# Feed-forward input as seven block products instead of eight: 19 gate/up pairs of a decoder layer in Strassen form

## The chip, the cores and the metric

One core of a Trainium2 chip runs the whole program. TensorE (PE in the profile) does the matmuls, VectorE (DVE) and ScalarE (ACT) the elementwise work, GpSimd (POOL) almost nothing, SyncE (SP) issues most DMAs. Matmuls write into PSUM, eight banks of 128 x 512 fp32 numbers; everything else lies in SBUF. Each engine works through its own queue in order and waits for others by semaphores. The metric is device time in microseconds.

## The reference

One hybrid decoder layer, fp32, 512 positions, width 1024: three token mixers, an output projection, and a gated feed-forward layer. The change touches the last, together with the norm ahead of it:

```
x = x + rms_norm(merged @ w_o, g_post_mix)
hf = rms_norm(x, g_pre_ffn)                        # 512 x 1024
f_gate, f_up = split(hf @ w_ffn_in, 2, axis=-1)    # 2816 columns each
f = (silu(f_gate) * f_up) @ w_ffn_out              # 2816 -> 1024
return x + rms_norm(f, g_post_ffn)
```

## The kernel before

Every large product is done in three passes: each fp32 operand is split into a high part in the matmul format fp32r and a low part (the rest), and high x high, high x low and low x high are summed in a bank. `split` (L114, L119) is a ScalarE copy into the high part and a VectorE subtraction for the low one. Weights come 128 x 1024 at a time: one DMA into a staging buffer, one split, then a unit of hi and lo tiles. `wlist` holds all weights in order, and `unit()` keeps three loaded ahead.

The program is written as Python generators that `run` interleaves; Tile, the layer below, then orders each engine's instructions by a model of its own and places the waits. The tail of the program runs so:

- `wo_pass` / `wo_norm` (L1014, L1027 to L1055): output projection for two of four row chunks at a time, then norm, residual, second norm, and four transposes per group through two `tr` banks into the transposed activations fh and fl. The second half of the norm runs while the next stage has begun.
- `ffn_head`: three gate/up pairs in two column halves, 256 of the 512 positions at a time, so that the first half can start before the norm of the second is done. 24 matmuls per unit and half.
- `ffn_tile`, 19 times: one pair, that is 128 gate and 128 up columns. 24 matmuls of 512 columns for the gate, 24 for the up part (8 blocks of the inner dimension x 3 passes, L212), each with its own weight load, in two banks. Then `ffn_out`: ScalarE Silu of the gate bank, VectorE product with the up bank, and a split of the result f.
- `down` (L1116): the output product, 22 units, with f as the loaded operand. It ends in `close`, which needs x for the residual.

Of the kernel before, what the change touches and what calls it, by code (L numbers as in the profile page):

```python
# [29 lines left out]
S = 512  # L30
# [20 lines left out]
def hybrid_block(ctx: ExitStack, tc: tile.TileContext, A, out):  # L51
# [23 lines left out]
    def next_phase(i):  # L75
        if phase[0]:
            phase[0].__exit__(None, None, None)
        phase[0] = tc.tile_pool(name=f"phase{i}", bufs=1, reuse_waits="tile")
# [16 lines left out]
    def row(name, dt=F32, tag="row"):  # L95
        return mid.tile([128, S], dt, tag=tag, name=nm(name), bufs={"row": 6, "q32": 2, "tg": 2}[tag])

# [61 lines left out]
    HEAD, LAST, LASTV = 3, 4, 2  # L159
    wlist += [(A["w_fi"][i], "h" if i < 4 else None) for i in range(2 * NFF)]  # L160
    wlist += [(A["w_fo"][i], "y" if 22 - LAST <= i < 20 else None) for i in range(22)]
    wready = {}
# [3 lines left out]
    def wload(upto):  # L166
        while wnext[0] < min(upto, len(wlist)):
            i = wnext[0]
# [38 lines left out]
    def passes(ps, hi, lo, xh, xl, m=128, n0=0, n1=S):  # L207

        t = 0
        for k in range(NK):  # L210
            for w, x in ((hi, xh), (hi, xl), (lo, xh)):
                res["mm"] = PE.matmul(ps[:m, n0:n1], w[:, k * 128:k * 128 + m], x[k][:, n0:n1], start=(t == 0),  # L212
                          stop=(t == 3 * NK - 1))
                t += 1
                if t % 6 == 0 and t < 3 * NK:
                    yield
# [742 lines left out]
    def gate_part(b, j):  # L959
        ps = bank("mm")  # L960
        yield from matrix(ps, hh, hl)
        t = row("tg", tag="tg")
        mg[b, j] = t
        SC.activation(t, ps, AF.Tanh, scale=0.5)
# [20 lines left out]
    def rows_in():  # L985
        gb = slab("gb", tag="gb", shape=(2, D))
        res["gb"] = gb
        SC.dma_start(gb[:, 0], bass.AP(tensor=A["grow"].tensor, offset=A["grow"].offset, ap=[[0, 128], [1, D]]))
        SC.dma_start(gb[:, 1], bass.AP(tensor=A["grow"].tensor, offset=A["grow"].offset + D,
                                       ap=[[0, 128], [1, D]]))  # L990
        V.tensor_scalar(gb[:, 0], gb[:, 0], 0.5, None, op0=OP.mult)
        xs = [slab("xr", tag="x", shape=(2, D)) for _ in range(2)]
        for i in range(2):
            SC.dma_start(xs[i], A["x"][:, 2 * i:2 * i + 2, :])
        res["x"] = [xs[c // 2][:, c % 2, :] for c in range(4)]
        res["ss"] = const.tile([128, 4, 4], F32, name="ss")
        res["fh"], res["fl"] = Pair("fh", F32R, "y"), Pair("fl", F32R, "y")

# [20 lines left out]
    def wo_norm(c0):  # L1019
# [24 lines left out]
        for _ in range({0: 9, 2: 14}[c0]):  # L1044
            yield 1
        for c in cs:
            for f in range(2):
# [5 lines left out]
                with tc.issue_after(res["mm"].ins):  # L1053
                    for i in range(4):
                        PE.transpose(pt[:, i * 128:(i + 1) * 128], n[:, i * 128:(i + 1) * 128], ident)  # L1055
                q = slice(c * 128, (c + 1) * 128)
                split(pt.rearrange("p (k t) -> p k t", k=4), res["fh"].t[f][:, :, q], res["fl"].t[f][:, :, q])
                for _ in range({0: 1, 2: 2}[c0]):
                    yield 1

    ff = {"h": [], "l": []}

    def ffn_out(j, pg, pu):

        if j % 2 == 0:
            ff["t"] = slab("f", F32R, (["m"] * 2 + ["mo"] * 4 + ["f"] + ["h"] * 4)[j // 2], (2, 2, S))
        ff["h"].append(ff["t"][:, j % 2, 0, :])
        ff["l"].append(ff["t"][:, j % 2, 1, :])
        s = row("silu")
        res["silu"] = SC.activation(s, pg, AF.Silu)  # L1070
        V.tensor_mul(s, s, pu)  # L1071
        split(s, ff["h"][j], ff["l"][j])

    def ffn_head(n):

        us, bs = [], []
        for i in range(2 * n):
            us.append(unit())
            bs.append(bank("mm"))
            yield from passes(bs[i], *us[i], res["fh"], res["fl"], n1=256)  # L1080
            yield
        for i in range(2 * n):
            yield from passes(bs[i], *us[i], res["fh"], res["fl"], n0=256)
            yield
            if i % 2:
                ffn_out(i // 2, bs[i - 1], bs[i])

    def ffn_tile(j):
        pg, pu = bank("mm"), bank("mm")
        yield from matrix(pg, res["fh"], res["fl"])  # L1090
        yield
        yield from matrix(pu, res["fh"], res["fl"])
        ffn_out(j, pg, pu)

    def down(f, last):
# [49 lines left out]
        for i in range(n - last):  # L1145
            hi, lo = unit()
            for c in range(4):
                block(c, i, hi, lo)
                yield
# [172 lines left out]
```

## Time and profile before

| | |
|---|---|
| median of 3 runs | 1148.39 us (1148.23 to 1148.74) |
| profiled execution: span, first to last instruction | 1146.6 us |
| busy: TensorE / its weight loads | 1133.5 us (99%) / 945.5 us (82%) |
| busy: VectorE / ScalarE / GpSimd | 689.8 us (60%) / 533.3 us (47%) / 24.0 us (2%) |
| 19 gate/up pairs, 813.35 to 1020.10 us | 206.75 us |

Each number on the page is one execution, and the span leaves out what lies around the instructions: 1.8 us between it and the median of the runs. In a group row the count stands behind the x, then busy time and mean time of one, then how long the engine stood idle ahead of them and for whom. Rows of a timeline begin with start and duration in us. A matmul's duration covers its way through the array; its successor starts before it ends, so the rate is read from the starts.

### The profile page before, as it was taken

What the parts mean: (1) busy time and instruction counts of PE and PEld (TensorE: products, weight loads), DVE (VectorE), ACT (ScalarE), POOL (GpSimd) and SP (SyncE); (2) the same over time, 40 slices, a digit from 0 to 9 for tenths busy, and PEclk for the clock granted to TensorE, in tenths of its full rate; (3) what the DMA queues carried; (4) which work ended last, traced back from release to release, by engine and by line L of the source; (5) the groups of instructions that cost most, each with busy time, mean ns of one, the idle gap of its engine ahead of it and who ended that gap; (6) DMA issues with size and microseconds to landing.
All of it is one profiled execution on the core that took longest, in us unless ns stands there. A gap on an engine that the chain in (4) does not pass through costs nothing.

```text
span 1146.6 us, 14314 instructions
## 1 busy us (share of the span) xinstructions
PE 1133.5 (99%) x5528; PEld 945.5 (82%) x5528; DVE 689.8 (60%) x1284; ACT 533.3 (47%) x934; POOL 24.0 (2%) x39
## 2 busy tenths in 40 slices
PE   9999999999999999999999999999999999999997
PEld 8888788888889888888788788889888888888886
DVE  5975968362675999989997734466333333332323
ACT  6746656132344787767777433343322232231221
POOL 1000022200000000000000000000000000000000
PEclk9999999999999999999999999999999999999999
DMA  8332223422223101111021432431223323332332
GB/s 314 100 109 74 92 92 112 182 83 101 86 80 93 59 34 56 56 56 56 19 74 56 149 127 92 141 114 40 74 92 101 101 92 93 105 115 92 95 108 73
DMA packets 30163, 108.61 MB, mean 95 GB/s; under 512 B 3536, under 2 KB 3824, under 8 KB 28944
## 3 DMA queue, kind: packets, MB, share of 16 engines
q1 hardware_dynamic: 27648, 97.98, 26.1%
q10 hardware_dynamic: 2160, 9.04, 2.2%
q8 instruction: 43, 0.70, 0.3%
q0 software_dynamic: 288, 0.69, 0.2%
q14 instruction: 24, 0.20, 0.1%
HBM read 105.60 MB, written 2.10 MB: 94 GB/s over the span
## 4 chain that ended last, share of the span: by engine, by line
PE 90%; DVE 6%; ACT 3%; DMA 1%; issue 1%; SPq 0%; DVEq 0%; ACTq 0%
PE mm L212 59%; PE mm L1116 10%; PE mm L496 3%; PE sc L808 3%; PE o L846 3%; PE tr L833 3%; PE mm L724 2%; PE mm L1014 2%; DVE lo L119 1%; PE tr L422 1%; DVE ti L449 1%; DMA raw<-in_w_v 1%; PE tr L556 1%; PE tr L640 1%; PE tr L746 1%
## 5 line engine op out<-in xcount | busy, mean ns | idle before, releaser
L114 ACT ACTIVATE hi<-raw 128x1024 fp32r<-128x1024 f32 (+1 forms) x162 | 170.8, 1054 | 352.6 <-PE mm L212 161.3
L119 DVE TENSOR_TENSOR lo<-raw,hi 128x1024 fp32r<-128x1024 f32 (+1 forms) x162 | 197.8, 1221 | 211.2 <-ACT hi L114 204.1
L212 PE MATMUL mm<-hh,hi 128*128 128x512 f32 x504 | 199.7, 396 | 0.0
L212 PE MATMUL mm<-hl,hi 128*128 128x512 f32 x504 | 197.4, 392 | 0.0
L212 PE MATMUL mm<-hh,lo 128*128 128x512 f32 x504 | 197.4, 392 | 0.0
L212 PE MATMUL mm<-fh,hi 128*128 128x512 f32 (+1 forms) x336 | 127.6, 380 | 0.0
L212 PE MATMUL mm<-fl,hi 128*128 128x512 f32 (+1 forms) x336 | 127.3, 379 | 0.0
L212 PE MATMUL mm<-fh,lo 128*128 128x512 f32 (+1 forms) x336 | 127.3, 379 | 0.0
L212 PEld LDWEIGHTS mm<-hh,lo 128*128 128x128 f32 x504 | 94.6, 188 | 19.7 <-issue 0.2
L212 PEld LDWEIGHTS mm<-hh,hi 128*128 128x128 f32 x504 | 94.7, 188 | 19.0 <-ACT hi L114 0.4
L212 PEld LDWEIGHTS mm<-hl,hi 128*128 128x128 f32 x504 | 94.7, 188 | 18.5 <-issue 0.2
L1116 PE MATMUL mm<-hi,f 128*128 128x512 f32 x320 | 99.2, 389 | 0.0
L814 ACT ACTIVATE P<-P,ast 128x128 f32<-128x128 f32 (+3 forms) x128 | 70.6, 554 | 23.1 <-DVE ast L812 22.5
L212 PEld LDWEIGHTS mm<-fl,hi 128*128 128x128 f32 x336 | 63.2, 188 | 11.9
L212 PEld LDWEIGHTS mm<-fh,lo 128*128 128x128 f32 x336 | 63.2, 188 | 11.9
L212 PEld LDWEIGHTS mm<-fh,hi 128*128 128x128 f32 x336 | 63.2, 188 | 11.7
L1116 PEld LDWEIGHTS mm<-hi,f 128*128 128x128 f32 x320 | 60.1, 188 | 12.4
L812 DVE CUSTOM_DVE_ANT_0 P<-sc,mask 128x128 f32<-128x128 f32 (+3 forms) x128 | 57.8, 483 | 8.3 <-PE sc L808 7.4
L1116 PE MATMUL mm<-lo,f 128*128 128x512 f32 x160 | 62.2, 389 | 0.0
L114 ACT ACTIVATE ph<-tr 128x512 fp32r<-128x512 f32 x80 | 46.9, 591 | 26.4 <-PE tr L833 25.5
L1071 DVE TENSOR_TENSOR silu<-silu,mm 128x512 f32<-128x512 f32 x22 | 15.1, 688 | 70.9 <-PE mm L212 70.9
L119 DVE TENSOR_TENSOR pl<-tr,ph 128x512 fp32r<-128x512 f32 x80 | 54.3, 685 | 2.9 <-PE o L846 1.0
(298 smaller groups left out, 1907.3 us busy)
## 6 DMA issues: line engine op xcount, KB each, us to landing
raw<-in_w_in SPq DMA_DIRECT2D x64, 512.0 KB, 3.5
raw<-in_w_fi SPq DMA_DIRECT2D x44, 512.0 KB, 3.5
raw<-in_w_br SPq DMA_DIRECT2D x24, 512.0 KB, 3.4
raw<-in_w_fo SPq DMA_DIRECT2D x22, 512.0 KB, 3.5
w<-in_cw ACTq DMA_DIRECT2D x4, 1024.0 KB, 5.0
raw<-in_w_o SPq DMA_DIRECT2D x8, 512.0 KB, 3.5
raw<-in_w_v SPq DMA_DIRECT2D x7, 512.0 KB, 5.2
xt<-in_xT SPq DMA_DIRECT2D x8, 256.0 KB, 6.7
```

What stands on the lines that cost most here:

```text
L114: SC.activation(hi, src, AF.Copy)
L119: res["lo"] = V.tensor_sub(lo, src, f32(hi))
L212: res["mm"] = PE.matmul(ps[:m, n0:n1], w[:, k * 128:k * 128 + m], x[k][:, n0:n1], start=(t == 0), stop=(t == 3 * NK - 1))
L496: res["mm"] = PE.matmul(b[c], x[k][:, c * 128:(c + 1) * 128], w[:, kk * 512:kk * 512 + 512], start=(k == 0 and t == 0), stop=(k == NK - 1 ...
L724: PE.matmul(ps, x[k][:, q], w[:, ws], start=(k == 0 and t == 0), stop=(k == NK - 1 and t == 2))
L808: PE.matmul(ps[:, :w * n].rearrange("p (b n) -> p b n", b=w), lhs, K[:, i, brs[0]:brs[-1] + 1, :n], start=(i == 0), stop=(i == 1))
L812: V.tensor_tensor_reduce(out=t, in0=ps[:, b * n:b * n + n], in1=mask[0][:, S - n:], scale=-0.125, scalar=3.0e38, op0=OP.add, op1=OP.min, a ...
L814: SC.activation(t, t, AF.Exp, scale=-1.0, bias=st[:, 0, j, b:b + 1], accum_out=st[:, 1, j, b:b + 1])
L833: PE.transpose(pt[:, j * 128:(j + 1) * 128], self.part(j, br)[:, kt * 128:(kt + 1) * 128], ident)
L846: PE.matmul(po, VV[:, kt, g % 2, br].rearrange("p i d -> p (i d)"), x, start=(br == 0 and kt == 0 and t == 0), stop=(br == 1 and kt == a a ...
L1014: res["mm"] = PE.matmul(b[c, f], x[k][:, q], w[:, fs], start=(k == 0 and t == 0), stop=(k == NK - 1 and t == 2))
L1116: PE.matmul(b[c], x[k][:, q], w[:, ws], start=(k == 0 and t == 0), stop=(k == NFF - 1 and t == 2))
```

## The change

Let the activations be a 2 x 2 block matrix A (position halves of 256 by inner halves of 512) and a pair's weights a 2 x 2 block matrix B (inner halves by gate and up). The product A B by blocks takes eight block products; the change computes it with seven (Winograd's form of Strassen's scheme): P1 to P7, each 512 inner x 256 positions x 128 columns, with block sums S1 to S4 of A (made once) and T1 to T4 of B (made for each pair). A product is 4 inner blocks x 3 passes = 12 matmuls of 256 columns. P1, P6, P5 and P3 add up in one bank, and P7 and P4 in another, P2 has a third. ScalarE copies the first bank after P1 (a), after P1+P6 (b) and after P1+P6+P5 (d), so that the four results are a + P2, b + P7 + P4, d + P7, and the bank itself.

The core of the diff:

```diff
+                if c0 == 0:
+                    SC.activation(F[f][:, :, q], p3, AF.Copy)
+                elif f == 0:
+                    SC.activation(F[2][:, :, q], p3, AF.Copy)
+                else:
+                    V.scalar_tensor_tensor(F[3][:, :, q], p3, -1.0, F[2][:, :, q], op0=OP.mult, op1=OP.subtract)
...
+        spill()
+        V.tensor_sub(F[2], F[0], F[2])
+        yield 1
+        V.scalar_tensor_tensor(F[0], F[3], -1.0, F[0], op0=OP.mult, op1=OP.subtract)
+        yield 1
+        V.tensor_sub(F[1], F[1], F[0])
+        yield 1
+        prep.load(HEAD)
+        prep.load(HEAD + 1)
+        for n, f in (("S3", 2), ("S2", 0), ("S1", 3), ("S4", 1)):
+            res[n] = slab(n, F32R, "mo", (2, 4, 256))
+            split(F[f], res[n][:, 0], res[n][:, 1])
+            yield 1
+        for step in prep.steps(HEAD):
+            step()
...
-    def ffn_out(j, pg, pu):
-        if j % 2 == 0:
-            ff["t"] = slab("f", F32R, (["m"] * 2 + ["mo"] * 4 + ["f"] + ["h"] * 4)[j // 2], (2, 2, S))
-        ff["h"].append(ff["t"][:, j % 2, 0, :])
-        ff["l"].append(ff["t"][:, j % 2, 1, :])
-        s = row("silu")
-        res["silu"] = SC.activation(s, pg, AF.Silu)
-        V.tensor_mul(s, s, pu)
-        split(s, ff["h"][j], ff["l"][j])
...
+            def b_pair():
+                split(r[0], *g["B11", "B21"])
+            def t13():
+                V.tensor_sub(T[:, 0], B["B11"], B["B12"])
+                V.tensor_sub(T[:, 1], B["B22"], B["B12"])
+            def t24():
+                V.tensor_add(T[:, 2], B["B22"], T[:, 0])
+                V.tensor_sub(T[:, 3], B["B21"], T[:, 2])
+            def s13():
+                split(T[:, 0:2, :].rearrange("p a n -> p (a n)"), *g["T1", "T3"])
+            def s22():
+                split(B["B22"], *g["B22"])
+            def s24():
+                split(T[:, 2:4, :].rearrange("p a n -> p (a n)"), *g["T2", "T4"])
...
+    PRODUCTS = {"P1": ("B11", (0, 0)), "P2": ("B21", (0, 1)), "P3": ("B22", "S4"), "P4": ("T4", (1, 1)),
+                "P5": ("T1", "S1"), "P6": ("T2", "S2"), "P7": ("T3", "S3")}
...
+            first = p in ("P1", "P7", "P2")
+            if first:
+                d[p] = bank("mm")[:, :256]
+            ps = d[{"P6": "P1", "P5": "P1", "P3": "P1", "P4": "P7"}.get(p, p)]
+            for k in range(4):
+                ks = slice(k * 128, k * 128 + 128)
+                for t, (w, l) in enumerate(((hi, 0), (hi, 1), (lo, 0))):
+                    res["mm"] = PE.matmul(ps, w[:, ks], x[:, l, k, :], start=(first and k == t == 0),
+                                          stop=(k == 3 and t == 2), skip_group_check=not first)
...
+        def keep(j, n):
+            SC.activation(st[j][n], st[j]["P1"], AF.Copy)
...
+            if name == "P1":
+                rows(j)
+                keep(j, "a")
+            elif name == "P6":
+                keep(j, "b")
+            elif name == "P5":
+                keep(j, "d")
+            elif name == "C11":
+                V.tensor_add(d["a"], d["a"], d["P2"])
+                SC.activation(d["a"], d["a"], AF.Silu)
+            elif name == "C22":
+                V.tensor_add(d["d"], d["d"], d["P7"])
+            elif name == "C12":
+                d["f"] = ffn_tile(j)
+                V.tensor_mul(d["f"][:, :256], d["a"], d["P1"])
+            elif name == "C21":
+                V.tensor_add(d["b"], d["b"], d["P7"])
+                res["silu"] = SC.activation(d["b"], d["b"], AF.Silu)
+                V.tensor_mul(d["f"][:, 256:], d["b"], d["d"])
...
+            last = j == j1 - 1
+            step(j, "P2")
+            step(j - 1, "P5")
+            step(j, "P1")
+            go()
+            step(j - 1, "C22")
+            step(j, "C11")
+            go()
+            step(j - 1, "P3")
+            step(j - 1, "C12")
+            go()
+            step(j, "P7")
+            go()
+            if not last:
+                step(j - 1, "P4")
+                step(j - 1, "C21")
+            go()
+            step(j, "P6")
...
+    def down_in(i):
+        if i >= NFF // 2:
+            return
+        f = ff["all"][i // 2][:, i % 2 * 2:i % 2 * 2 + 2, :].rearrange("p a n -> p (a n)")
+        u = slab("fs", F32R, (["m", "gb"] + ["h"] * 4 + ["mo"] * 4 + ["m"])[i], (2, 2, S))
+        split(f, *(u[:, l].rearrange("p a n -> p (a n)") for l in range(2)))
...
-    run([ffn_tile(j) for j in range(HEAD, NFF)])
+    ffn_fast(HEAD, NFF)
```

`go` takes one of the six weight steps of the next pair (`b_pair` to `s24`) at a time. `ffn_fast` runs `step` for pairs 3 to 21; a product left over from the pair ahead (j - 1) comes between those of pair j. f is kept in fp32, and `down_in` splits it two tiles at a time inside `down`. x goes out to DRAM after the second norm (`spill`, four transfers on SyncE's queue), its buffers hold f tiles, and it comes back during `down` (`unspill`). In `wo_norm` each transposed group is copied once more in fp32 for the block sums (L1086, L1088, L1090), S1 to S4 are formed and split, and the first pair's weights are prepared there. The head works as before from differently laid out tiles. Two sets of weight tiles alternate between pairs: hi_1180 to lo_1185 and g_1186 to g_1189.

Tile's order moves instructions far from where they are written. First ScalarE, one pair in the middle of the 19 (L114 is the copy of a split, L1070 the Silu; before):

```order
L1070 ACTIVATE silu_1243_7494<-mm_1234_7431 128x512 [waits PE_49]
L114 ACTIVATE hi_1247_7503<-raw_1246_7501 128x1024
L114 ACTIVATE f_1242_7493<-silu_1243_7494 128x512 [waits DVE_49]
L114 ACTIVATE hi_1250_7533<-raw_1249_7531 128x1024
L1070 ACTIVATE silu_1252_7561<-mm_1244_7499 128x512 [waits PE_49]
```

and now, where L1245 is the bank copy, fx holds a and b, fy holds d, L117 is the copy of a split, T the block sums, L1262 and L1270 the Silus of C11 and C21:

```order
L1245 ACTIVATE fx_1251_8049<-mm_1250_8036 128x256 [waits PE_49]
L117 ACTIVATE hi_1182_7013<-T_1190_7021 128x1024 [waits PE_49,Activation_49]
L1245 ACTIVATE fy_1252_8050<-mm_1250_8036 128x256 [waits PE_49]
L117 ACTIVATE g_1186_7017<-raw2_1254_8121 128x1024 [waits DMAHW2_49,PE_49,Activation_49]
L1245 ACTIVATE fx_1257_8163<-mm_1256_8150 128x256 [waits PE_49,Activation_49]
L117 ACTIVATE g_1189_7020<-raw_1248_8007 128x512 [waits DMAHW1_49,PE_49]
L1262 ACTIVATE fx_1257_8163<-fx_1257_8163 128x256 [waits DVE_49]
L117 ACTIVATE hi_1184_7015<-T_1190_7021 128x1024 [waits PE_49]
L1270 ACTIVATE fx_1251_8049<-fx_1251_8049 128x256 [waits DVE_49]
L1245 ACTIVATE fx_1257_8163<-mm_1256_8150 128x256 [waits PE_49]
```

Four operations a pair became nine, and the weight copy into hi_1182 (T1 and T3 of the pair behind mm_1256's, into the tile that P5 of the older pair reads) now stands between the bank copies b and d of one pair.

Second TensorE at the same place. S1 marks P5 of the older pair (bank mm_1250, weights hi_1182 and lo_1183), A_1005 with bank mm_1256 is P1 of the newer one, S4 is P3 of the older one, S3 is P7 of the newer one:

```order
L1236 MATMUL mm_1250_8036<-S1_1176_6989,hi_1182_7013 128x256 x2
L1236 MATMUL mm_1250_8036<-S1_1176_6989,lo_1183_7014 128x256
L1236 MATMUL mm_1256_8150<-A_1005_5766,g_1186_7017 128x256 [waits DVE_49]
L1236 MATMUL mm_1256_8150<-A_1005_5766,g_1186_7017 128x256 x11
L1236 MATMUL mm_1250_8036<-S4_1177_6998,g_1189_7020 128x256 [waits Activation_49]
L1236 MATMUL mm_1250_8036<-S4_1177_6998,g_1189_7020 128x256 x11
L1236 MATMUL mm_1259_8188<-S3_1174_6971,g_1187_7018 128x256 [waits DVE_49]
```

Before, a bank was filled by 24 matmuls and read only after the last; now the bank mm_1250 is read between its products, and P3 waits for ScalarE.

Third VectorE over the same pair (L122 is the subtraction of a split, L1261 to L1271 the sums and products of C11 to C21, L1197 and L1198 the block sums T1 and T3):

```order
L122 TENSOR_TENSOR lo_1183_7014<-T_1190_7021,hi_1182_7013 128x1024 [waits PE_49,Activation_49]
L1264 TENSOR_TENSOR fy_1252_8050<-fy_1252_8050,mm_1253_8074 128x256 [waits Activation_49]
L122 TENSOR_TENSOR g_1186_7017<-raw2_1254_8121,g_1186_7017 128x1024 [waits DMAHW2_49,PE_49,Activation_49]
L1261 TENSOR_TENSOR fx_1257_8163<-fx_1257_8163,mm_1255_8124 128x256 [waits Activation_49]
L1267 TENSOR_TENSOR f_1239_7841<-fx_1251_8049,mm_1250_8036 128x256 [waits PE_49]
L122 TENSOR_TENSOR g_1189_7020<-raw_1248_8007,g_1189_7020 128x512 [waits Activation_49]
L1197 TENSOR_TENSOR T_1190_7021<-raw2_1254_8121 128x512 [waits DMAHW3_49,DVE_49]
L1198 TENSOR_TENSOR T_1190_7021<-raw2_1254_8121 128x512
L1269 TENSOR_TENSOR fx_1251_8049<-fx_1251_8049,mm_1253_8074 128x256 [waits PE_49]
L122 TENSOR_TENSOR lo_1185_7016<-T_1190_7021,hi_1184_7015 128x1024 [waits Activation_49]
L1271 TENSOR_TENSOR f_1239_7841<-fx_1251_8049,fy_1252_8050 128x256 [waits Activation_49]
```

Where it had two weight subtractions, a product and one more subtraction for each pair, it now has thirteen operations (the two that make T2 and T4 follow), and the addition L1269, on which the second Silu waits, stands ninth.

More of the change, by code (lines that the diff above doesn't have):

```diff
@@ L95, in row @@
     def row(name, dt=F32, tag="row"):
-        return mid.tile([128, S], dt, tag=tag, name=nm(name), bufs={"row": 6, "q32": 2, "tg": 2}[tag])
+        pool, bufs = phase_pool[tag] if tag in phase_pool else (mid, 6)
+        return pool.tile([128, S], dt, tag=tag, name=nm(name), bufs=bufs)
     def bank(tag):
@@ L213, in passes, with half_passes @@
                           stop=(t == 3 * NK - 1))
+                t += 1
+                if t % 6 == 0 and t < 3 * NK:
+                    yield
+    def half_passes(ps, hi, lo, i):
+        t = 0
+        n = slice(256 * i, 256 * i + 256)
+        for k in range(NK):
+            x = res["A"][i, k // 4]
+            for w, l in ((hi, 0), (hi, 1), (lo, 0)):
+                res["mm"] = PE.matmul(ps[:, n], w[:, k * 128:k * 128 + 128], x[:, l, k % 4, :], start=(t == 0),
+                                      stop=(t == 3 * NK - 1))
                 t += 1
@@ L1045, in wo_norm @@
             yield 1
+        if c0 == 0:
+            fx = [slab("xf", tag=t, shape=(2, 4, 256)) for t in ("fx", "f")]
+            res["F"] = [fx[i // 2][:, i % 2] for i in range(4)]
+        F = res["F"]
         for c in cs:
@@ new lines, in spill, with unspill, ffn_tile @@
+    def spill():
+        d = tc.dram_tile([4, 128, D], F32, name="x1")
+        res["x1"] = d
+        for c in range(4):
+            SY.dma_start(d[c], res["x"][c])
+    def unspill(c):
+        if c == 0:
+            xs = [slab("xr", tag="x", shape=(2, D)) for _ in range(2)]
+            res["x"] = [xs[c // 2][:, c % 2, :] for c in range(4)]
+        SY.dma_start(res["x"][c], res["x1"][c])
+    ff = {"t": [], "all": []}
+    def ffn_tile(j):
+        if j % 4 == 0:
+            ff["s"] = slab("f", tag=("m", "fx", "f", "x", "x", "y")[j // 4])
+            ff["all"].append(ff["s"])
+        ff["t"].append(ff["s"][:, j % 4, :])
+        return ff["t"][j]
@@ L1079, in ffn_head @@
             bs.append(bank("mm"))
-            yield from passes(bs[i], *us[i], res["fh"], res["fl"], n1=256)
+            yield from half_passes(bs[i], *us[i], 0)
             yield
         for i in range(2 * n):
-            yield from passes(bs[i], *us[i], res["fh"], res["fl"], n0=256)
+            yield from half_passes(bs[i], *us[i], 1)
             yield
             if i % 2:
[L1086 to L1093, printed above, removed]
+                s, f = row("silu"), ffn_tile(i // 2)
+                res["silu"] = SC.activation(s, bs[i - 1], AF.Silu)
+                V.tensor_mul(f, s, bs[i])
```

110 lines of the change are left out of this document (101 added, 9 removed).

## The prediction

> **What bounds the kernel now.** I read the page first (busy shares, then the chain that ended last), then the chain in order of time for the last third, then busy time by stretch, then single rows for durations.
>
> ```profile
> span 1146.6 us, 14314 instructions
> PE 1133.5 (99%) x5528; PEld 945.5 (82%) x5528; DVE 689.8 (60%) x1284; ACT 533.3 (47%) x934; POOL 24.0 (2%) x39
> PE 90%; DVE 6%; ACT 3%; DMA 1%; issue 1%; SPq 0%; DVEq 0%; ACTq 0%
> ...
> 796.12 224.14 PE mm L212 x1056
> 1020.26 119.69 PE mm L1116 x528
> ```
>
> TensorE is on the chain for 90% of the span, and from 796 to 1140 us the chain is nothing else. So the feed-forward input is worth what its matmuls cost, as long as nobody makes TensorE wait. A "busy" PE does not say at what rate it works; the starts of consecutive matmuls do.
>
> ```profile
> 813.11 0.28 PE L212 MATMUL mm<-fl,hi 128*128 128x256 f32 x1
> 813.23 0.28 PE L212 MATMUL mm<-fh,lo 128*128 128x256 f32 x1
> 813.35 0.40 PE L212 MATMUL mm<-fh,hi 128*128 128x512 f32 x1
> ...
> 1020.10 0.39 PE L1116 MATMUL mm<-hi,f 128*128 128x512 f32 x1
> ...
> core 0: us, PE busy (x) PEld busy (x) DVE busy (x) ACT busy (x) POOL busy (x), PEclk, DMA share, GB/s
> 813.35:1020.10 206.75, 206.75 (x914) 171.18 (x913) 71.91 (x78) 61.29 (x78) 0.00 (x0) 1.00 0.32 102
> 783.00:813.35 30.35, 30.35 (x256) 30.29 (x255) 13.79 (x30) 10.39 (x19) 0.00 (x0) 1.00 0.00 1
> ```
>
> The 19 pairs run from 813.35 to 1020.10 us at the full granted clock (1.00): 206.75 us for 19 x 48 = 912 matmuls of 512 columns, **0.2267 us** each, 10.88 us a pair. The head just ahead runs 256-column matmuls with a weight load each, as the new code will: their starts are **0.120 us** apart (813.11, 813.23, 813.35). Both are columns / 2400 per us plus 0.0133 us, so halving the columns does not quite halve the time. VectorE works 71.91 us in this stretch (35%), ScalarE 61.29 us (30%): 3.8 and 3.2 us a pair.
>
> **The change part by part.**
>
> *Matmuls.* A pair goes from 48 matmuls of 512 columns to seven products of 4 x 3 = 12 matmuls of 256 columns, 84 in all: 84 x 0.120 = 10.08 us against 10.88. Columns fall by 12.5%, time by 7.4%, because 36 more matmuls each pay the 0.0133 us. Over 19 pairs: 1596 x 0.120 = 191.5 us for 206.75, a gain of **15.2 us**. It is the ceiling of the change.
>
> *VectorE and ScalarE.* The rows:
>
> ```profile
> L119 DVE TENSOR_TENSOR lo<-raw,hi 128x1024 fp32r<-128x1024 f32 x160 | 196.4, 1228 | 211.0 <-ACT hi L114 203.8 <-PE tr L556 6.0 <-PE o L846 0.7
> L1071 DVE TENSOR_TENSOR silu<-silu,mm 128x512 f32<-128x512 f32 x22 | 15.1, 688 | 70.9 <-PE mm L212 70.9
> L737 DVE TENSOR_TENSOR V<-mm,V 128x256 fp32r<-128x256 f32 x8 | 3.4, 422 | 1.0 <-ACT V L736 0.9
> L114 ACT ACTIVATE hi<-raw 128x1024 fp32r<-128x1024 f32 x160 | 169.5, 1059 | 350.2 <-PE mm L212 161.3 <-issue 104.1 <-PE mm L1116 60.4
> L381 ACT ACTIVATE gs<-gs 128x512 f32<-128x512 f32 x16 | 10.1, 628 | 12.6 <-DVE gs L380 12.6
> L736 ACT ACTIVATE V<-mm 128x256 fp32r<-128x256 f32 x8 | 3.0, 388 | 4.4 <-DVE V L737 2.2 <-PE mm L724 1.3 <-PE o L846 0.9
> ```
>
> Per pair VectorE gets three residues of 1024 (3 x 1.228), four block sums and one residue of 512 (5 x 0.69) and five operations of 256 (5 x 0.42): 9.23 us of duration. ScalarE gets three copies of 1024 (3.18), one of 512 (0.63), three bank copies of 256 (1.16) and two Silus of 256 (0.41 each, estimated from the 1059 and 628 ns rows: 431 ns less per 512 columns, so half of that under 628): 5.8 us. So VectorE, a third busy before, becomes 90% busy. That by itself costs nothing; an in-order queue this full does if something TensorE needs stands late in it. Operations that wait for nothing start before the one ahead has ended:
>
> ```profile
> 772.58 1.23 DVE L119 TENSOR_TENSOR lo<-raw,hi 128x1024 fp32r<-128x1024 f32 x1 [1.35 <-ACT hi L114]
> 773.72 1.28 DVE L119 TENSOR_TENSOR fl<-tr,fh 128x512 fp32r<-128x512 f32 x2
> 774.92 1.27 DVE L1029 TENSOR_TENSOR yg<-mm,gb 128x512 f32<-128x512 f32 x2
> ...
> 884.12 1.06 ACT L114 ACTIVATE hi<-raw 128x1024 fp32r<-128x1024 f32 x1 [3.84 <-PE mm L212]
> 885.09 0.58 ACT L1070 ACTIVATE silu<-mm 128x512 f32<-128x512 f32 x1
> ...
> 885.22 1.23 DVE L119 TENSOR_TENSOR lo<-raw,hi 128x1024 fp32r<-128x1024 f32 x1 [3.61 <-ACT hi L114]
> ```
>
> A 1024 operation holds VectorE 1.14 us (772.58 to 773.72), a 512 one 0.60, ScalarE's copy 0.97 (884.12 to 885.09); the next engine starts 0.04 us after an end (885.18, 885.22).
>
> *The handback on the accumulation bank.* P1, P6, P5, P3 add up in one bank, and ScalarE copies the running sum after each of the first three; the next product into the bank must wait. By the order of products three others lie between P1 and P6 and one between the later ones, 12 x 0.120 = 1.44 us. ScalarE's queue over one pair, shown with the change, decides whether 1.44 us is enough. Let t = 0 be the first matmul of P1 of the pair with bank mm_1256; the pair ahead has mm_1250.
>
> ScalarE's copy after P5 (into fy_1252) stands behind a 1024-column weight copy that overwrites hi_1182, the high part of the weights of that same P5. The weight copy may not start until P5's eleventh matmul, the last reader of hi_1182, is through, and P3 (S4 in TensorE's rows there), only P1 further on, waits for the bank copy behind it. That matmul starts at -0.24 and ends 0.28 later, at 0.04. Weight copy from 0.08, the bank copy from 1.05 (+ 0.97) to 1.44 (+ 0.388), seen at 1.48. What a late product loses:
>
> ```profile
> 795.85 0.19 PEld L212 LDWEIGHTS mm<-fh,u 128*128 128x128 f32 x1
> 795.88 0.37 PE L212 MATMUL mm<-fh,u 128*128 128x256 f32 x1
> 795.96 0.19 PEld L212 LDWEIGHTS mm<-fl,u 128*128 128x128 f32 x1
> 796.08 0.28 PE L212 MATMUL mm<-fl,u 128*128 128x256 f32 x1
> ```
>
> In the stream a load starts 0.12 us ahead of its matmul (795.96, 796.08); behind a break the second matmul comes 0.23 us after the first load, as in the stream. So P3 loses what its load is late: due at 1.44 - 0.12 = 1.32, free at 1.48, **0.16 us** a pair. All later products stand behind P3 in TensorE's order, so it is paid in full. It meets about 17 of the 19 pairs: 2.7 us. Bounds: nothing (were the order of the two copies harmless) and 0.4 us, should ScalarE run each at full duration (1.06) with waits of 0.1 us between engines, 6.8 us in all.
>
> *The second edge.* The copy after P6 must be done 0.12 us before P5. By now TensorE is 0.16 us on: P6's first matmul starts at 5.92 and its last ends at 7.52; P5's load is due at 8.68. Ahead of that copy ScalarE has the Silu of the older pair, which waits for VectorE's addition (L1269). VectorE's queue up to it, at full durations: residue of T (from 0.08 + 1.06 + 0.04 = 1.18) 1.23, sum 0.42, residue 1.23, 0.42, 0.42, 0.69, two block sums 0.69 each, addition 0.42, so 6.2 us, to 7.4; Silu to 7.85, copy to 8.25. That is 0.4 us early even without overlap; with it VectorE is at 6.7 and the copy waits for P6. I put it at nothing; if VectorE's durations were longer, it costs one for one.
>
> *The way in.* In the first half of the output projection's norm, four transposed groups share two banks. ScalarE now copies each group twice (L1086, 0.6 us) and the second copies stand behind others. The fourth group already waits for VectorE:
>
> ```profile
> 774.45 0.42 PEld L1055 LDWEIGHTS tr<-ident,xn 128*128 128x128 f32 x4 [0.64 <-DVE fl L119]
> 774.46 0.65 PE L1055 MATMUL tr<-ident,xn 128*128 128x128 f32 x4 [0.21 <-DVE fl L119]
> ```
>
> One or two 0.6 us copies more put it back by 0 to 1.3 us; I take **0.7**. The block sums S1 to S4 and the first pair's weights, seven operations of 1024 more and 7.1 us of weight work, 15.7 us of VectorE, fall into the head, where it was busy 13.79 of 30.35 us. What overruns it is the first pair's last residue (T2, T4), needed at P6, three products or 4.3 us on.
>
> *Covered.* Writing x out and back moves 2 MB each way, four 512 KB transfers. In the head the DMA share is 0.00; if the queue stood in the way, a transfer is 3.5 us (the page's DMA issues). Splitting f moves to the output stage: eleven 1024 pairs (1.06 on ScalarE, 1.23 on VectorE), one per 24 matmuls of 0.2267 = 5.44 us, beside one weight split of the same size: 2.5 of 5.4 us on VectorE. Nothing is hung on them at either end; uncovered, the first split is 2.3 us.
>
> *Sum.* -15.2 + 2.7 + 0.7 = **-11.8 us**: the profiled span of 1146.6 becomes 1134.8. The runs' median, 1148.39, lies 1.8 us above the span; the same on top gives **1136.6 us**.
>
> The Trainium skill ("TensorE: Matmul & The Clock Gate", Back-to-back issue gap) gives N / 2.4 + 2.5 ns between matmuls, 215.8 and 109.2 ns; by it 912 and 1596 of them cost 196.8 and 174.3 us, a gain of 22.5 us before waits. The trace has 226.7 and 120 ns for fp32r with a load each, so the measurement decides.
>
> **The rivals.**
>
> 1. *No handback wait.* If ScalarE is ready a little earlier than I count, the whole 15.2 us stays: 1133.2. For it: my margin is 0.16 us. Against: the row order is fixed.
> 2. *Larger waits.* Handback of 0.4 us a pair (the upper bound), and a way in of 1.3: -15.2 + 6.8 + 1.3 = -7.1, 1141.3. For it: ScalarE and VectorE are chained many times a pair.
> 3. *VectorE becomes the bound, slower than before.* Its operations can be longer than their form's usual time:
>
> ```profile
> L119 DVE TENSOR_TENSOR ycl<-yc,ych x8: 683/896/1107, 138.7 to 202.5; 128x512 fp32r<-128x512 f32 x8
> POOL 1000022200000000000000000000000000000000
> ```
>
> 896 ns at the median for a 690 ns form, 1.3 times. Then the chain to L1269 takes 8.1 us instead of 6.2, the Silu ends at 9.75 and the bank copy at 10.15; P5 is 1.5 us late, a pair takes 10.08 + 0.16 + 1.5 = 11.7 us, and 19 x 0.86 + 0.7 puts the run at 1165. It decides from 18% on: there the pair is back at 10.88. Against: those slow rows lie where GpSimd works, which is idle in the last thirty slices, and all other rows here have 685 to 690.
> 4. *Nothing gained:* waits of about 0.8 us a pair eat it up, VectorE 18% longer.
> 5. *The full rate of 109 ns:* -22.5 + 2.7 + 0.7 gives 1129. The head's rows speak against it.
>
> **How the numbers follow.** Forecast 0.58; no wait 0.11; larger waits 0.14; VectorE the bound 0.09; nothing gained 0.05; full rate 0.03. A difference of 0.2% (2.3 us) is about what can be told from none here. Faster: 0.58 + 0.11 + 0.14 + 0.03 = 0.86; same 0.05; slower 0.09. Range: from the ceiling, 1133, to rival 2 and a little, 1143; it leaves out 0.17.
>
> **What would show it.** In the new profile starts of 256-column matmuls in L1236 are 0.12 us apart and pairs 10.2 us; TensorE's largest wait there is for ScalarE's copy into fy (L1245), some 17 times 0.1 to 0.2 us. VectorE is about 90% busy in the stage, waiting at the T residues, not TensorE for it. Pairs of 10.08 mean rival 1; over 10.5, or TensorE waiting ahead of P5, rival 2 or 3; a matmul spacing other than 0.12 overturns the ceiling itself.

## The result, and the profile after

The changed kernel takes 1138.16 us (median of 4 runs, 1137.12 to 1139.09) against 1148.57 us (1148.23 to 1149.11) for the kernel before, taken beside it: a ratio of 0.9908, 95% interval 0.9894 to 0.9922. The forecast was 1136.6. The profiled execution took 1138.17 us around a span of 1136.0.

The page of the changed kernel: the span, the busy shares, and the chain by engine.

```profile
span 1136.0 us, 16012 instructions
PE 1121.7 (99%) x6212; PEld 967.1 (85%) x6212; DVE 797.4 (70%) x1472; ACT 592.0 (52%) x1047; POOL 24.0 (2%) x39
...
PE 88%; DVE 6%; ACT 3%; DMA 1%; issue 1%; DVEq 0%; ACTq 0%
```

TensorE still ends last. The span is 10.6 us shorter with 684 more matmuls. The chain in order of time says where the 10.6 us lie (start, duration, what):

```profile
815.13 191.56 PE mm L1236 x1572
1006.69 0.69 PE mm L1341 x3
1007.39 2.90 PE mm L1236 x24
1010.29 119.04 PE mm L1341 x525
```

The new stage (L1236) is one piece of TensorE, as the old one was; three matmuls of the output stage (L1341) stand in it. I cut the run at three TensorE rows: the first matmul of the output projection (730.98 us before, 731.09 after), the first of the stage (813.35 and 814.97) and the end of stage and output stage together (1139.95 and 1129.33, a matmul's tail aside). Upstream +0.1 us; the **way in** 82.37 to 83.88, +1.5; **stage and output stage** 326.60 to 314.36, -12.2; the tail after that is the same. Sum -10.6. So the stage gave what was forecast (-12.5) and the way in cost twice what was forecast (+0.7).

What the other engines do in the stage, busy time by stretch (columns as on the same view before):

```profile
core 0: us, PE busy (x) PEld busy (x) DVE busy (x) ACT busy (x) POOL busy (x), PEclk, DMA share, GB/s
815.20:1006.00 190.80, 190.80 (x1568) 188.76 (x1567) 160.32 (x244) 107.58 (x173) 0.00 (x0) 1.00 0.32 102
```

VectorE is busy for 84% of it (35% before), ScalarE for 56%, at the full granted clock. The place where a little is lost, in single rows around one P3; the first two are ScalarE's, the next two TensorE's weight loads, the last three its matmuls:

```profile
854.45 1.06 ACT L117 ACTIVATE g<-T 128x1024 fp32r<-128x1024 f32 x1 [2.44 <-PE mm L1236]
855.42 0.36 ACT L1245 ACTIVATE fy<-mm 128x256 f32<-128x256 f32 x1
...
855.51 0.19 PEld L1236 LDWEIGHTS mm<-A,lo 128*128 128x128 f32 x1
855.83 0.53 PEld L1236 LDWEIGHTS mm<-S,g 128*128 128x128 f32 x4
...
855.39 0.40 PE L1236 MATMUL mm<-A,hi 128*128 128x256 f32 x2
855.63 0.28 PE L1236 MATMUL mm<-A,lo 128*128 128x256 f32 x1
855.84 0.74 PE L1236 MATMUL mm<-S,g 128*128 128x256 f32 x4
```

ScalarE's 1024-column weight copy waits 2.44 us for the last reader of its target, then holds the engine from 854.45 to 855.42; the copy of the bank into fy follows and ends at 855.78; TensorE's next load starts at 855.83, 0.32 us after the one ahead of it instead of 0.12. It is the handback wait of the forecast, at the place named there. By the starts of the matmuls it meets 15 of the 19 pairs, 0.18 us each (a pair takes 10.26 us instead of 84 x 0.120 = 10.08). TensorE's waits on the way in (waited for: us in total, times, longest):

```profile
PE mm L229 <- ACT A L117: 0.6, 1, 0.6
PE tr L1081 <- ACT xf L1086: 0.4, 1, 0.4
PE tr L1081 <- DVE xn L1076: 0.4, 1, 0.4
```

Before there was one, of 0.2 us, for VectorE's fl. The second row is the one that I had priced; the first and the third are new. The experiments take the two stretches apart.

### The profile page after: what moved, and what is told of

Same layout as the page of the kernel before. It is cut to its first block, busy times and chain, and to the rows that moved or that the text cites. A ratio compares the mean times of both kernels' runs of the same rounds, so it can differ in the third digit from the quotient of the medians.

```text
span 1136.0 us, 16012 instructions
## 1 busy us (share of the span) xinstructions
PE 1121.7 (99%) x6212; PEld 967.1 (85%) x6212; DVE 797.4 (70%) x1472; ACT 592.0 (52%) x1047; POOL 24.0 (2%) x39
## 4 chain that ended last, share of the span: by engine, by line
PE 88%; DVE 6%; ACT 3%; DMA 1%; issue 1%; DVEq 0%; ACTq 0%
PE mm L216 38%; PE mm L1236 17%; PE mm L1341 11%; PE mm L513 4%; PE o L863 3%; PE sc L825 3%; PE tr L850 3%; PE mm L741 2%; PE mm L229 2%; PE mm L1036 2%; DVE lo L122 1%; PE tr L439 1%; DVE ti L466 1%; DMA raw<-in_w_fi 1%; PE tr L573 1%
## 5 line engine op out<-in xcount | busy, mean ns | idle before, releaser
L122 DVE TENSOR_TENSOR lo<-raw,hi 128x1024 fp32r<-128x1024 f32 (+1 forms) x132 | 161.0, 1220 | 135.4 <-ACT hi L117 128.2
L117 ACT ACTIVATE hi<-raw 128x1024 fp32r<-128x1024 f32 (+1 forms) x132 | 138.9, 1053 | 202.3 <-PE mm L216 81.8
L1341 PE MATMUL mm<-hi,fs 128*128 128x512 f32 x288 | 89.5, 389 | 0.0
L1236 PE MATMUL mm<-S,g 128*128 128x256 f32 x552 | 73.8, 286 | 0.0
L1236 PEld LDWEIGHTS mm<-S,g 128*128 128x128 f32 x552 | 68.5, 191 | 2.2 <-ACT fy L1245 0.2
L1341 PEld LDWEIGHTS mm<-hi,fs 128*128 128x128 f32 x288 | 54.1, 188 | 11.2
L117 ACT ACTIVATE ph<-tr 128x512 fp32r<-128x512 f32 x80 | 46.9, 591 | 26.3 <-PE tr L850 25.4
L122 DVE TENSOR_TENSOR pl<-tr,ph 128x512 fp32r<-128x512 f32 x80 | 54.4, 685 | 2.8 <-PE o L863 1.0
L1341 PE MATMUL mm<-lo,fs 128*128 128x512 f32 x144 | 56.0, 389 | 0.0
L825 PE MATMUL sc<-K,q 128*128 128x512 f32 (+2 forms) x192 | 50.8, 367 | 0.0
L850 PE MATMUL tr<-ident,P 128*128 128x128 f32 x320 | 48.9, 273 | 0.3 <-DVE pl L122 0.2
L850 PEld LDWEIGHTS tr<-ident,P 128*128 128x128 f32 x320 | 39.0, 140 | 10.4 <-DVE pl L122 1.5
L1236 PE MATMUL mm<-S,hi 128*128 128x256 f32 x240 | 44.5, 283 | 0.0
L1236 PE MATMUL mm<-A,hi 128*128 128x256 f32 x240 | 44.4, 283 | 0.0
```

The source lines that it names most:

```text
L117: SC.activation(hi, src, AF.Copy)
L122: res["lo"] = V.tensor_sub(lo, src, f32(hi))
L825: PE.matmul(ps[:, :w * n].rearrange("p (b n) -> p b n", b=w), lhs, K[:, i, brs[0]:brs[-1] + 1, :n], start=(i == 0), stop=(i == 1))
L850: PE.transpose(pt[:, j * 128:(j + 1) * 128], self.part(j, br)[:, kt * 128:(kt + 1) * 128], ident)
L1236: res["mm"] = PE.matmul(ps, w[:, ks], x[:, l, k, :], start=(first and k == t == 0), stop=(k == 3 and t == 2), skip_group_check=not first)
L1341: PE.matmul(b[c], x[k][:, q], w[:, ws], start=(k == 0 and t == 0), stop=(k == NFF - 1 and t == 2))
```

## The experiments

In the kernels below the first matmul of the output projection starts between 730.7 and 732.0 us, though nothing ahead of it was edited; I take this for scatter between executions. So each kernel is judged by its way in and its stage (first matmul of the stage to the end of its last, just ahead of the bulk of the output stage: 195.32 us in the changed kernel; the expectations' 194.5 goes by starts, 0.16 us less, and leaves out the 0.7 us of three foreign matmuls) and by the ratio of its runs. Tile, the layer that orders the instructions, can answer an edit with another order elsewhere; where the traces show that, it is said.

**1. The weight copy behind the bank copy.** Only the order of two instructions in ScalarE's queue changes.

```diff
-            SC.activation(st[j][n], st[j]["P1"], AF.Copy)
+            res["k" + n] = SC.activation(st[j][n], st[j]["P1"], AF.Copy)
...
             def s13():
+                if "kd" in res:
+                    with tc.issue_after(res["kd"].ins):
+                        split(T[:, 0:2, :].rearrange("p a n -> p (a n)"), *g["T1", "T3"])
+                    return
```

> Only ScalarE's order changes: the copy of the T1/T3 weights is queued behind the bank copy after P5 instead of ahead of it. Theory (the recorded one): P3 is late only because the 0.97 us weight copy stands ahead of the bank copy. Then TensorE's restarts at P3 go, 17 to 18 pairs at 0.16 to 0.18 us, the stage from the first L1236 matmul to the first of the output stage falls from 194.5 to about 191.6 us, and the run from 1138.2 to about 1135.3. Rival: reading a bank that goes on accumulating costs its restart whatever the order; then the stage stays at 194.5 and the run at 1138.2. Second rival: the weight copy, now about 0.4 us later, puts VectorE's residue of T and the addition for the second Silu back, so that P5 or the next pair's P6 waits; then half or more of the gain comes back as waits ahead of P5 and the run is 1136.5 to 1138.

Measured: 1135.67 us, ratio 0.9886 [0.9869, 0.9902]. Stage 192.52 us, 2.8 less; way in 83.97, unchanged. Of TensorE's restarts in the stage only one of 0.1 us, in the first pair, is left. ScalarE's rows at the same point of the pair, and the chain:

```profile
855.12 0.39 ACT L1249 ACTIVATE fy<-mm 128x256 f32<-128x256 f32 x1 [2.50 <-PE mm L1240]
855.40 1.05 ACT L117 ACTIVATE g<-T 128x1024 fp32r<-128x1024 f32 x1
...
816.09 188.75 PE mm L1240 x1572
```

The bank copy now waits for the matmuls alone and ends 0.59 us behind the first matmul of P1 (854.92) instead of 1.47 (855.78 after 854.31 above); the weight copy behind it makes nothing late. So the wait was the queue order, not the bank: 2.8 us, and the theory's 2.9. What is left without the three foreign matmuls is 191.8 us, 191.7 by starts: 1596 x 0.1201.

**2. Plain block products.** Eight products instead of seven, 96 matmuls a pair, no weight sums, and no bank that is read before all its matmuls are done; what lies around the pairs is as in the changed kernel.

```diff
-            return [b_pair, t13, t24, s13, s22, s24]
+            return [b_pair, lambda: split(r[1], *g["T1", "T3"])]
...
+            for i, n in enumerate((("B11", "B21"), ("T1", "T3"))):
+                b.append(bank("mm"))
+                for h in range(2):
+                    for _ in half_passes(b[i], *prep.g[j][n], h):
+                        pass
```

> The 19 pairs as plain block products: per pair 96 matmuls of 256 columns into two banks that are each written once, no weight sums, no bank copies, no additions; everything around it (halved activations, the block sums, written-out x, fp32 f) as in the changed kernel. Theory: 256 columns cost 0.120 us whatever the product, 1824 x 0.120 = 218.9 us for the stage, 24.4 more than the 194.5 now; run about 1162.5, 14 slower than before the change. If a matmul without a handback near it ran at 0.109 us, the stage would be 199 and the run 1143. If the smaller columns alone carried waits of their own (weights of 128 columns not loaded in time), the stage would be above 220.

Measured: 1161.98 us, ratio 1.0117 [1.0102, 1.0132]. The chain has the head's last 144 and the stage's 1824 matmuls, all of 256 columns, in one piece:

```profile
797.26 236.28 PE mm L229 x1968
```

0.1201 us each. So 0.120 us holds with and without a bank that is read between its products. And it is the product saved that makes the change faster: with the same columns and eight products the program is 13.4 us slower than the kernel before. The Trainium skill's isolated gap ("TensorE: Matmul & The Clock Gate", Back-to-back issue gap), 109.2 ns by its formula, which was a rival here, is not what the 3,500 matmuls of these two runs show.

**3. The writes of x from another queue.** On the way in, first the queue was suspected.

```diff
-            SY.dma_start(d[c], res["x"][c])
+            GP.dma_start(d[c], res["x"][c])
```

> Only the queue changes from which the four writes of x are issued: GpSimd's instead of SyncE's, where they stand between the weight loads. Theory Q: on the way in (first matmul of the output projection to the first of the stage, 83.9 us now, 82.4 before the change) the 0.6 us wait of a head matmul for ScalarE's A comes from a weight that arrives late behind those writes. Then this wait goes, the way in falls by 0.5 to 0.9 us, the run to about 1137.4. Rival X: it is the third read of the transposed banks by ScalarE that holds them; then the way in stays within 0.2 us of 83.9 and the run at 1138.2. Nothing else of the stage should move (194.5 us).

Measured: 1138.87 us, ratio 0.9915 [0.99, 0.993]; way in 84.08. Theory Q missed; the number is the rival's. DMA issues from 745 to 775 us (KB each, median us from issue to landing), of before, the changed kernel, and this one:

```profile
raw<-in_w_fi SPq DMA_DIRECT2D x7, 512.0 KB, 3.5
```

```profile
raw<-in_w_fi SPq DMA_DIRECT2D x6, 512.0 KB, 4.2
x<-xr SPq DMA_DIRECT2D x2, 512.0 KB, 5.5
```

```profile
raw<-in_w_fi SPq DMA_DIRECT2D x7, 512.0 KB, 4.1
x<-xr POOLq DMA_DIRECT2D x2, 512.0 KB, 4.7
```

Two of the four writes go in the idle head (786.43 and 787.76 us in the changed kernel), but two do not. They go at 759.58 and 762.04 us, as soon as the first two chunks of x are final, among the loads of the head's weights; 4.46 MB instead of 3.54 move in those 30 us, and a load takes 4.1 to 4.2 us at the median from whichever queue the writes come. That is what the Trainium skill says ("DMA: Bandwidth & Descriptors", Issuing engines are not separate DMA queues): another issuing engine saves only the time to issue. By the medians the trace agrees, but they hide the chain. In the changed kernel the three loads among the writes take 4.1, 5.6 and 4.6 us, the three in their place before 3.4, 3.5 and 3.5. The second one lands 2.2 us late, VectorE does four operations of the norm (xn) ahead of its residue (three of them in the chain below), and the load of the last head weight waits for that residue. The chain before and now:

```profile
766.02 1.22 DVE u L119
767.27 4.18 DMA raw<-in_w_fi
```

```profile
767.39 2.07 DVE xn L1076 x3
769.46 1.15 DVE u L122
770.62 3.46 DMA raw<-in_w_fi
```

Here is what the late load does in the changed kernel (timeline, ScalarE and TensorE):

```profile
773.05 0.60 ACT L1086 ACTIVATE xf<-tr 128x512 f32<-128x512 f32 x1 [1.28 <-DVE A L122]
774.10 1.06 ACT L117 ACTIVATE hi<-raw 128x1024 fp32r<-128x1024 f32 x1 [0.45 <-DMA raw<-in_w_fi]
775.07 0.58 ACT L117 ACTIVATE A<-tr 128x512 fp32r<-128x512 f32 x1
...
776.76 0.50 PE L229 MATMUL mm<-A,u 128*128 128x256 f32 x2 [0.58 <-ACT A L117]
777.70 0.66 PE L1081 MATMUL tr<-ident,xn 128*128 128x128 f32 x4 [0.44 <-ACT xf L1086]
```

The last head weight is copied at 774.10 (771.48 before), and the second group's copy into A, transposed at 772.36, stands behind it. With the writes on GpSimd the three loads take 3.4, 4.4 and 4.3 us and the weight comes 1.8 us earlier, at 772.28. But the edit also changed Tile's order: the split of this weight now stands ahead of the first group's into A, on ScalarE and on VectorE, and the next wait is there, for the bank:

```profile
774.52 0.68 DVE L122 TENSOR_TENSOR A<-tr,A 128x512 fp32r<-128x512 f32 x1
775.24 0.60 ACT L1086 ACTIVATE xf<-tr 128x512 f32<-128x512 f32 x1 [1.41 <-DVE A L122]
775.89 0.66 PE L1081 MATMUL tr<-ident,xn 128*128 128x128 f32 x4 [1.24 <-ACT xf L1086]
```

The third read starts 0.04 us after VectorE's residue ends (775.20, 775.24; in the changed kernel 773.01, 773.05 too): a transposed bank is read three times in a row, not by two engines at once.

**4. The third read taken away.** High and low part are added again in SBUF, by GpSimd.

```diff
-                if c0 == 0:
-                    SC.activation(F[f][:, :, q], p3, AF.Copy)
...
+                d = F[c0 + f][:, :, q]
+                GP.tensor_add(d, f32(a[:, 0, :, q]), f32(a[:, 1, :, q]))
```

> The fp32 copies for the block sums are no longer read out of the transposed banks by ScalarE (L1086) or VectorE; GpSimd adds high and low part from SBUF instead, so a bank is free after the residue. Theory X (the recorded one for the way in): the third reads held the two banks; the waits of the transposes behind xf go, ScalarE loses 3 copies of 0.6 us, the way in falls from 83.9 by 0.4 to 1.0 us, the run to about 1137.4. Rival Q (the writes of x delay the weight loads): within 0.2 us of 83.9, run 1138.2. If GpSimd's additions slow VectorE beside them, as the 896 ns rows of the profile before suggest for other operations, the way in could be longer by up to 1 us instead.

Measured: 1139.02 us, ratio 0.9921 [0.9906, 0.9936]; way in 84.80, worse by 0.9. The wait for xf is gone, but the late weight is still there (its residue stands ahead of the second group's into A on VectorE, as in the changed kernel), and the second norm is later too (TensorE's rows, and GpSimd's addition):

```profile
772.17 1.28 POOL L1086 TENSOR_TENSOR xf<-A 128x512 f32<-128x512 f32 x1 [532.82 <-DVE A L122]
776.64 0.66 PE L1081 MATMUL tr<-ident,xn 128*128 128x128 f32 x4 [0.87 <-DVE A L122]
791.61 0.63 PE L1081 MATMUL tr<-ident,xn 128*128 128x128 f32 x4 [1.05 <-DVE xn L1076]
```

Neither of the two edits gained anything alone, and in each trace the other suspect's wait is still there.

**5. The writes of x later**, behind the last load of the first two pairs, from the same queue as in the change.

```diff
-        spill()
         V.tensor_sub(F[2], F[0], F[2])
...
         prep.load(HEAD + 1)
+        with tc.issue_after(res["ld"].ins):
+            spill()
...
+                res["ld"] = SY.dma_start(r[i], A["w_fi"][2 * j + i])
```

> Only the place of the four writes of x changes: behind the last weight load of the first two pairs, instead of among the loads for the head while the output projection still runs. Moving them to another queue alone had left the way in at 84.2 us. Theory C: the writes share the memory path with the weight loads (4.2 us a load in that stretch against 3.5 before the change), which puts the last head weight 2.6 us back, and ScalarE's copy of that weight stands ahead of its second copy into A. Then loads take 3.5 us again, that weight copy starts 1.5 to 2.6 us earlier, TensorE's 0.6 us wait for A goes; the transposes' wait behind the third read (xf) stays or grows to at most 1.2, so the way in is 83.2 to 83.8 instead of 84.0 and the run 0.2 to 0.8 faster. Rival: the time of the loads is not what matters, only ScalarE's and VectorE's extra work; way in 84.0.

Measured: 1137.14 us, ratio 0.9903 [0.9889, 0.9917]; way in 83.40, 0.5 less, at the expected place. The loads, the weight copy and TensorE's one remaining wait:

```profile
raw<-in_w_fi SPq DMA_DIRECT2D x7, 512.0 KB, 3.7
```

```profile
771.50 1.06 ACT L117 ACTIVATE hi<-raw 128x1024 fp32r<-128x1024 f32 x1 [1.48 <-DMA raw<-in_w_fi]
```

```profile
PE tr L1081 <- ACT xf L1086: 0.6, 1, 0.6
```

The weight is back at its old time, 2.6 us earlier, and TensorE does not wait for A. On the way in TensorE, ScalarE and VectorE follow the order of run 3 here, so against run 3 it is the writes beside the loads that are gone: the wait for xf is 0.57 us instead of 1.24, the way in 83.40 instead of 84.08. By the ratios the run gains 0.6 us on the changed kernel, which the intervals don't tell from nothing. The way in does: 83.40, and 83.47 in run 9, against 83.88 to 83.98 in the four kernels that leave it as in the change (the change itself, runs 1, 7 and 8).

**6. Late writes, and the first norm's third reads on GpSimd.**

> The late writes of the run above, and the first norm's four third reads (L1086) replaced by additions of high and low part on GpSimd. Theory: the way in has two causes, late loads and the third read holding a bank, each hidden behind the other when only one is taken away. With both gone the way in is back at 82.4 to 82.8 us, where it was before the change, the run 1136.6 to 1137.0. Rival: ScalarE and VectorE have simply more to do in this stretch; then the way in stays above 83.4 and the wait only moves on to xn or A, as it did with the third reads alone taken away (85.0).

Measured: 1137.58 us, ratio 0.9904 [0.9888, 0.9919]; way in 83.17. Less than expected: TensorE waits 0.4 us for A in the middle of the head (for VectorE), 0.2 for xn. Two of its runs took 1136.8 us and two 1138.4, the profiled one among these. The same order of ScalarE, VectorE and SyncE on the way in gave 82.62 in run 10 below, so with these edits a single trace tells the stretch to some 0.5 us, and the 0.2 us between this run and run 5 are not shown.

**7. and 8. More work for VectorE.** The last weight sum is done two or four times more, to the same values; each is one 512-column operation (three passes of the loop, or five).

```diff
-                V.tensor_sub(T[:, 3], B["B21"], T[:, 2])
+                for _ in range(3):
+                    V.tensor_sub(T[:, 3], B["B21"], T[:, 2])
```

> VectorE gets two more operations of 512 columns a pair: the last weight sum (T4) is done three times, to the same values, ahead of the addition for the second Silu. 1.2 us a pair of VectorE's time, 13% of its 9.23. Theory of the recorded chain: it is 0.4 us early at full durations and about 1.1 with overlapping starts, so P5 is late by 0.1 to 0.8 us a pair: the stage 194.5 grows by 2 to 15 us, run 1140 to 1153. Rival: VectorE may fall behind within a pair and only its sum counts, 10.26 less the 8.1 us that it is held, 2.2 us to spare: then nothing, 1138 +- 0.7.

> Four such extra operations a pair, 2.4 us of VectorE's time, 26% of its 9.23. By the recorded chain (decides from 18%, 1.7 us, on) P5 is 1.3 to 2.0 us late in every pair: the stage grows by 20 to 30 us and the run, 1160 to 1168, is slower than before the change. Rival: only the sum of VectorE's time counts, 8.1 + 2.4 = 10.5 us against a pair of 10.26: 0.2 to 0.4 us a pair, 4 to 8 us, run 1142 to 1146, still faster than before.

Measured: with two, 1137.38 us, ratio 0.9906 [0.9892, 0.9919], stage 195.46. Six foreign matmuls stand in this stage instead of three, so I take it together with the output stage: 313.81 us, where the changed kernel has 314.36. With four, 1144.12 us, ratio 0.9962 [0.995, 0.9975], stage and output stage 320.8: 6 us slower than the changed kernel, and still faster than before. Busy time by stretch, of the one with two, then of the one with four:

```profile
815.20:1006.00 190.80, 190.60 (x1575) 189.29 (x1574) 183.93 (x282) 106.79 (x174) 0.00 (x0) 1.00 0.31 104
```

```profile
815.20:1010.00 194.80, 192.62 (x1555) 187.96 (x1554) 193.03 (x312) 102.13 (x168) 0.00 (x0) 1.00 0.30 95
```

At 96% busy VectorE costs nothing; at 99% it has nothing to spare. By the starts of P3 from 867.20 to 992.61 us a pair then takes 10.41 to 10.51 us instead of 10.26, 2.3 us over those twelve pairs. Two waits at the end of the stage cost 2 us more, where the splits of f join the queue (TensorE):

```profile
1008.16 0.50 PE L1237 MATMUL mm<-S,hi 128*128 128x256 f32 x2 [0.66 <-ACT hi L117]
1009.42 0.39 PE L1237 MATMUL mm<-S,lo 128*128 128x256 f32 x1 [0.76 <-DVE lo L122]
```

Both times are the ones that the sum of VectorE's time gives. They are no test of the forecast's chain within a pair, though. The extra operations (L1203 below) were meant to stand ahead of the addition for the second Silu (L1270). Tile put all of them behind it, with four from 849 us on and with two from 914 us on, where VectorE stood idle for 1.49 us in the changed kernel; before that some stand ahead, but weight residues have moved behind instead. VectorE's rows in the changed kernel and in the run with two:

```profile
855.54 1.23 DVE L122 TENSOR_TENSOR g<-T,g 128x1024 fp32r<-128x1024 f32 x1 [1.49 <-ACT g L117]
```

```profile
962.40 0.41 DVE L1270 TENSOR_TENSOR fx<-fx,mm 128x256 f32<-128x256 f32 x1
...
965.40 2.15 DVE L1203 TENSOR_TENSOR T<-raw,T 128x512 f32<-128x512 f32 x3
```

Tile's order differs elsewhere too. With two, ScalarE stands idle ahead of the bank copies from 834 to 885 us, and P3 loses nothing there, as in run 1. With four, P3 follows P5 after four matmuls instead of twelve in the later pairs and starts 0.3 us late, waiting for the bank copy. How much of the 6 us is a full VectorE and how much this order is not shown.

**9. Queue order and late writes together.**

> Weight copy behind the bank copy, and the writes of x behind the loads. Theory: the two causes lie in different stretches and add up, 2.8 us in the stage (194.5 to 195.3 before, 192.5 alone) and 0.5 us on the way in (83.9, 83.4 alone): run 1138.2 - 3.3 = 1134.9, 0.5 to 0.8 under the first alone. Rival: what is saved on the way in is lost again at the head of the stage, since the first pair's last residue is not ready sooner; then 1135.7.

Measured: 1134.47 us, ratio 0.9882 [0.9865, 0.9898]; way in 83.47, stage 192.52. Both pieces are there, each as large as alone.

**10. The same, with the first norm's third reads on GpSimd.**

> As the run of both, and the first norm's third reads on GpSimd from SBUF. Theory: 0.2 us more on the way in (83.2 alone): 1134.6. Rival: GpSimd's additions of 1.28 us each slow VectorE beside them, so that A or the second norm comes later: 1134.9 or worse.

Measured: 1134.2 us, ratio 0.9879 [0.9864, 0.9894]; way in 82.62, stage 192.52.

**11. The same as 9, with one read of each transposed bank.** ScalarE copies the bank out once, and the split reads that copy.

```diff
+                if c0 == 0:
+                    SC.activation(F[f][:, :, q], p3, AF.Copy)
+                    p3 = F[f][:, :, q]
                 split(p3, a[:, 0, :, q], a[:, 1, :, q])
```

> As the run of both, but in the first norm ScalarE reads each transposed bank once, into the fp32 copy, and high and low part are made from that copy in SBUF: the bank is free 0.6 us after the transposes instead of after three reads in a row, with no work added on any engine. Theory (the third read holds the bank): the transposes' wait of 0.6 us goes, way in 82.6 to 83.1, run 1134.2 to 1134.6. Rival: A comes 0.6 us later on ScalarE's queue and a head matmul waits for it instead; way in 83.4 or more, run 1134.9 or more.

Measured: 1133.86 us, ratio 0.9876 [0.9861, 0.989]; way in 83.13, stage 192.53. The lowest of all, 14.3 us under the kernel before and, by the two ratios to it, 3.7 us under the changed kernel. Each theory was half right: the transposes do not wait for xf any more, and the head waits for A instead.

```profile
PE mm L229 <- ACT A L117: 0.9, 1, 0.9
```

Runs 9, 10 and 11 lie within 0.6 us and their intervals overlap, so which of them is best is not shown. That they are under the changed kernel is shown by the stage, 2.8 us shorter in each, and for run 11 by the intervals too.

## Why the prediction was right, and where it was wrong

*The ceiling, -15.2 us.* Right. The stage without its waits is 191.7 us by starts, against the 191.5 of the forecast (run 1), and 0.120 us a matmul held in two more kernels. That was the largest term, and it was read off matmuls of the same size that stood in the old profile.

*The handback, +2.7 us.* Right in place, cause and size: 2.8 us, gone when ScalarE's two copies change places. The copy into fy ended 1.47 us behind P1's first matmul, against 1.44 worked out from row durations. That the total fits to 0.1 us is partly luck: 15 pairs at 0.18 us, where the forecast had about 17 at 0.16.

*The second edge, nothing.* Right, and for the reason given. VectorE's addition, ScalarE's copy after P6 and TensorE's first load of P5, in a pair whose P1 starts at 844.05:

```profile
850.36 0.41 DVE L1269 TENSOR_TENSOR fx<-fx,mm 128x256 f32<-128x256 f32 x1
851.63 0.39 ACT L1245 ACTIVATE fx<-mm 128x256 f32<-128x256 f32 x1 [0.19 <-PE mm L1236]
852.75 0.91 PEld L1236 LDWEIGHTS mm<-S,g 128*128 128x128 f32 x7
```

The addition ends 6.7 us behind P1, which is the forecast's figure with overlap; the copy waits for P6 and not for the Silu, and it ends 0.73 us ahead of the load. A pair's VectorE work could grow by 1.2 us at no cost (run 7), but not inside this chain, so how much longer the chain itself may be was not tried.

*VectorE 90% busy.* It is 84%. The forecast added durations; operations that wait for nothing overlap, and busy time counts the overlap once.

*The way in, +0.7 us.* The wrong term: it cost 1.5. The part that was priced, the third reads holding two banks, is there (0.4 to 0.6 us of TensorE's wait). What failed is the step *Covered*, which put the writes of x at nothing because the DMA share in the head is 0.00. The number is right, but it holds for two of the four writes only. The other two are issued at 759.6 and 762.0 us, before the head begins (776.8) and beside its weight loads, since Tile sends them as soon as their data are final. The loads among them take 4.1 to 5.6 us instead of 3.4 to 3.5, the last weight comes 2.6 us late, and ScalarE's queue hands that on to A. Sending the writes later gave back 0.5 us (run 5). The forecast's own "if the queue stood in the way" looked for the harm in a queue. Run 3 took the writes out of that queue, which brought the weight 1.8 us earlier and gained nothing; runs 3 and 5, alike in order, differ by 0.7 us through the transfers themselves.

*The split of f and reading x back, nothing.* Right: the output stage is 119.73 us, against 119.69.

*Sum.* -11.8 forecast, -10.6 measured between the spans: 0.3 in the stage, 0.8 on the way in, 0.1 upstream that no edit made.

*The rivals.* No handback wait (1133.2) is where the kernel lands once the order is mended: run 1, and with the way in 1133.9. Of the larger waits the handback stayed at its forecast, and the way in, 1.5 us, came out above the 1.3 named there. VectorE as the bound did not come either: its operations had their usual lengths and the chain its room. Run 8 filled VectorE's queue and cost 6 us, not the 20 or more that its expectation drew from the chain; but most of the work was added behind the chain, so what slower operations inside it would cost, and with that the price of this rival, stays untested. Also open is the last 0.3 to 0.7 us of the way in, which a single trace doesn't resolve.

## What to carry to other kernels

Price a matmul rewrite from the starts of matmuls of the new size in the old profile, then look at each bank that is read while it goes on accumulating: what stands ahead of that copy in the copying engine's queue is paid on every round, and swapping two instructions gave back 2.8 us here. A write that "fits into an idle stretch" must be placed by when its data are final, not by where it stands in the source; look at the transfers that it will fly beside. And where taking away one suspect gains nothing, compare the order of the queues before dropping it: the edit may have moved another wait into the same place.

## What the runs showed of the hardware that I had not expected

Two 512 KB writes raised the median time of the 512 KB loads around them from 3.5 to 4.2 us, and to 4.1 when another engine issued them. With VectorE busy for 96% of the stage (run 7) no wait of TensorE for it shows. Adding two 128x512 fp32 tiles in SBUF took GpSimd 1.28 us, where VectorE's residues of that size take 0.68.
